# Emission order of attention groups and recurrence steps in an RWKV-7 layer

## The chip, the cores and the metric

One Trainium2 chip; the kernel runs on one of its cores. The metric is the time of one execution on the device, in microseconds (us), as the median of several runs. PE is the matrix engine (its weight loads are listed apart, as PEld), DVE the vector engine, ACT the scalar engine, POOL the general-purpose one, and SP the queue that issues nearly all DMAs here.

## What is computed

The reference runs a first block on a 256 x 1024 input (feed-forward, a mixer of two branches, feed-forward) and then a second block of two layers. The change lies in the mixer of the first block alone:

```python
h = rms_norm(x, mix_norm[l])
p_rwkv, p_q, p_k, p_v, p_gate = _split_last(h @ w_in[l], ...)
y_a = rwkv7_time_mix(p_rwkv, ...)        # a recurrence over 256 steps, 16 heads
y_b = dilated_attention(p_q, p_k, p_v, q_gain, k_gain)   # 3 groups of 4 heads, dilations 1, 4, 16
g_a, g_b = _split_last(jax.nn.sigmoid(p_gate + b_gate[l]), (D_MODEL, D_MODEL))
merged = g_a * (y_a @ w_proj_rwkv[l]) + g_b * (y_b @ w_proj_attn[l])
x = x + merged @ w_out[l]
```

The three attention groups are mixed at the end by a softmax over their log-sum-exp values, so `y_b` is complete only when the third group is. Until both branches are there nothing of them depends on the other.

## The kernel before

All matrices are float32, each split into a high and a low part, so that a product takes three matmuls (`gemm`, L214 to L216, with tokens on the partitions; `gemm_t`, L249 to L251, transposed). `weights` loads a piece, ACT casts its high part (L202) and DVE subtracts for the low one (L203).

The mixer is written as Python generators; each `yield` ends a step, and a string called `PLAN` says whose next step is emitted:

- `0` and `1` are the recurrence of the first and the second half of the heads (`rwkv_half`). Its steps: three of preparation; the Gram products (L689); four that share a chain of 31 pairs of small DVE operations (L718, L720), here s0-4, s5-10, s11-17 and s18-30; the inverse's other blocks (L736, L741); then for each half t of the tokens a step p (L790, L800), a step RG (L815) and two chunk steps ch (L839, L845). ch2 also holds the first normalization. Two more steps, the second normalization with its transposes (L309) and the last transposes, end a half.
- `k` is the second half's keys, `g` the gate chunks (`gate_work`, two of eight chunks a step; its results go to DRAM).
- `a` is `fill`: the attention's values; then for a group g its preparation (a `gemm`, squares, an inverse root by seven to ten tiny DVE operations in a chain, L285 to L290, and transposes, L911) and six steps of a three-stage pipeline over its four heads: `scores` (L923 to L931), `turn` (L937), `values` (L945 to L949). After group 2 come the softmax over groups (L962 to L972) and the transposes of the result (L309); then what is left of `g`, then the attention's projection (`project`, four chunks, L1007).

When the string ends, `for x in "0k1ga"` emits what is left of each, in that order. `last_projection` (the recurrence's projection and `w_out`) follows.

Emission order is a priority, not the order of an engine: the framework under the kernel places the semaphores and fixes each engine's order when the program is built, and lets later work go first where it expects earlier work to wait. The buffers are shared by tag: four PSUM banks `g` for dense products, four `t` for everything else on PE, 21 SBUF slots `q` and 16 slots `h`. Attention scores, masks' sums, gate values and normalization squares are all `h`; scores, transposes, values and every product of the recurrence are `t`. `ada` (L1162) is work for the second block, whose pool takes the memory that the recurrence frees.

Of the kernel before, what the change touches and what calls it, by code (L numbers as in the profile page):

```python
# [18 lines left out]

PLAN = "0000k000aa0000kk0010g010a0111gaa11aaa1aaa111a1aa11aa11a1aa"
P = 128
NQ, NH, NG, NWR, NWS, NS = 21, 16, 4, 4, 3, 2
D = 1024
# [106 lines left out]
class Builder:  # L132
# [890 lines left out]
    def first_block(self, X, nxt):  # L1023
# [29 lines left out]
        with self.inner() as self.ip:  # L1053
# [34 lines left out]
            for hh in range(2):  # L1088
                fills[str(hh)] = self.rwkv_half(hh, S[hh], yT)
            for x in PLAN:  # L1090
                next(fills[x], None)
# [592 lines left out]
```

## Time and profile before

| | us |
|---|---|
| median of 3 runs | 2926.4 (2920.22 to 2927.43) |
| profiled execution, its own time | 2930.7 |
| its span, first to last instruction | 2928.9 |
| PE busy | 2823.6 (96%) |
| DVE busy | 1933.8 (66%) |
| ACT busy | 1176.4 (40%) |
| granted PE clock, mean | 0.978 |

[...] Idle time of an engine counts only where later work waits for it.

### The profile page before, as it was taken

To read this page: it belongs to the slowest core of one execution; us is meant where nothing else is said; L and a number is where in the kernel's file an instruction comes from. 1 tells how busy PE (TensorE), PEld (TensorE's weight loads), DVE (VectorE), ACT (ScalarE), POOL (GpSimd) and SP (SyncE) were. 2 spreads that over 40 slices of the span, in tenths; PEclk is the share of its full clock that TensorE was granted. 3 is DMA by queue.
4 is the path that set the end of the run, shared out by engine and by line. 5 is a ranking of instruction groups with operands and counts; after the bars stand their busy time and mean duration, and the time that the engine had idled before them with its cause. 6 is when DMAs were issued, how large, how long until landed. Compare 5 with 4: busy or idle time off the path is not lost.

```text
span 2928.9 us, 42526 instructions
## 1 busy us (share of the span) xinstructions
PE 2823.6 (96%) x16536; PEld 2407.4 (82%) x16536; DVE 1933.8 (66%) x3478; ACT 1176.4 (40%) x1955; POOL 22.4 (1%) x81
## 2 busy tenths in 40 slices
PE   8999898899999999999999999999999999999998
PEld 7987777688987889877888878787778897799797
DVE  8867887868665544357764597777755456665656
ACT  4445344344444333244523333232334444444443
POOL 0000000000000000000000000000000000000000
PEclk9999897799999999999999999999999999999999
DMA  8756543466651222322152464454432342245564
GB/s 276 232 163 210 174 129 97 138 211 209 194 173 45 70 65 65 103 72 62 46 171 91 157 230 148 157 175 151 156 97 80 101 140 87 87 148 181 165 189 148
DMA packets 298644, 409.59 MB, mean 140 GB/s; under 512 B 31557, under 2 KB 182981, under 8 KB 298442
## 3 DMA queue, kind: packets, MB, share of 16 engines
q1 hardware_dynamic: 298442, 406.87, 43.9%
q8 instruction: 130, 2.13, 0.3%
q14 instruction: 72, 0.59, 0.1%
HBM read 396.98 MB, written 3.24 MB: 137 GB/s over the span
## 4 chain that ended last, share of the span: by engine, by line
PE 80%; DVE 13%; ACT 3%; DMA 2%; issue 2%; SPq 0%; DVEq 0%; ACTq 0%
PE g L215 12%; PE g L216 12%; PE g L214 11%; PE g L249 10%; PE g L251 10%; PE g L250 10%; DVE wl L203 3%; PE dC L1370 2%; PE tr L309 1%; PE I L1346 1%; DVE aa L1162 1%; ACT dae L1467 1%; ACT wh L202 1%; PE ada L1147 1%; PE f L1537 1%
## 5 line engine op out<-in xcount | busy, mean ns | idle before, releaser
L203 DVE TENSOR_TENSOR wl<-wr,wh 128x1024 fp32r<-128x1024 f32 (+1 forms) x606 | 733.1, 1212 | 581.8 <-ACT wh L202 579.6
L202 ACT CAST wh<-wr 128x1024 fp32r<-128x1024 f32 (+1 forms) x606 | 631.3, 1043 | 1056.4 <-PE g L216 490.6
L215 PE MATMUL g<-wl,xh 128*128 128x512 f32 (+2 forms) x1880 | 731.2, 389 | 21.6 <-DVE wl L203 21.0
L214 PE MATMUL g<-wh,xh 128*128 128x512 f32 (+2 forms) x1880 | 729.1, 391 | 5.7 <-ACT wh L202 4.6
L249 PE MATMUL g<-xh,wh 128*128 128x256 f32 (+1 forms) x2352 | 724.9, 308 | 3.2 <-DVE gate L1009 2.5
L216 PE MATMUL g<-wh,xl 128*128 128x512 f32 (+2 forms) x1880 | 726.2, 387 | 0.6 <-DVE xl L297 0.6
L251 PE MATMUL g<-xh,wl 128*128 128x256 f32 (+1 forms) x2352 | 720.7, 307 | 2.6 <-DVE wl L203 2.6
L250 PE MATMUL g<-xl,wh 128*128 128x256 f32 (+1 forms) x2352 | 720.4, 306 | 0.0
L249 PEld LDWEIGHTS g<-xh,wh 128*128 128x128 f32 x2352 | 450.8, 192 | 37.6 <-issue 12.2
L251 PEld LDWEIGHTS g<-xh,wl 128*128 128x128 f32 x2352 | 450.4, 192 | 26.5 <-DVE wl L203 3.4
L250 PEld LDWEIGHTS g<-xl,wh 128*128 128x128 f32 x2352 | 450.8, 192 | 20.9 <-issue 1.3
L215 PEld LDWEIGHTS g<-wl,xh 128*128 128x128 f32 x1880 | 358.7, 191 | 95.2 <-DVE wl L203 28.7
L214 PEld LDWEIGHTS g<-wh,xh 128*128 128x128 f32 x1880 | 355.9, 190 | 86.5 <-issue 9.2
L216 PEld LDWEIGHTS g<-wh,xl 128*128 128x128 f32 x1880 | 358.4, 191 | 72.2 <-DVE xl L297 3.7
L1162 DVE SCALAR_TENSOR_TENSOR aa<-wa,cond,aa 128x512 f32<-128x512 f32 x336 | 232.1, 745 | 6.8 <-DMA wa<-in_w_ada_dram 6.7
L296 ACT CAST xh<-tr 128x256 fp32r<-128x256 f32 (+1 forms) x114 | 50.6, 463 | 132.1 <-PE tr L309 124.0
L1467 ACT ACTIVATE dae<-sc,dast 128x512 f32<-128x512 f32 (+1 forms) x96 | 58.5, 614 | 42.2 <-DVE dast L1465 37.3
L297 DVE TENSOR_TENSOR xl<-tr,xh 128x256 fp32r<-128x256 f32 (+1 forms) x114 | 58.0, 530 | 21.6 <-ACT xh L296 21.3
L1465 DVE TENSOR_REDUCE dast<-sc 128x1 f32<-128x512 f32 (+1 forms) x96 | 53.8, 595 | 24.2 <-PE sc L1464 23.7
L1370 PE MATMUL dC<-vo,kw 128*128 128x257 f32 x192 | 50.3, 394 | 0.0
L309 PE MATMUL tr<-ident,hn 128*128 128x128 f32 x160 | 26.7, 305 | 24.4 <-DVE hn L357 17.5
L1162 DVE SCALAR_TENSOR_TENSOR aa<-wa,cond,ab 128x512 f32<-128x512 f32 x48 | 34.9, 746 | 20.1 <-PE ada L1147 16.7
(387 smaller groups left out, 2537.0 us busy)
## 6 DMA issues: line engine op xcount, KB each, us to landing
wr<-in_w_in_dram SPq DMA_DIRECT2D x156, 512.0 KB
wa<-in_w_ada_dram SPq DMA_DIRECT2D x192, 256.0 KB
wr<-in_ffn_w_in_dram SPq DMA_DIRECT2D x88, 512.0 KB
wr<-in_w_ffn_in_dram SPq DMA_DIRECT2D x84, 512.0 KB
wr<-in_w_in_dram SPq DMA_DIRECT2D x156, 256.0 KB
wr<-in_w_ffn_out_dram SPq DMA_DIRECT2D x50, 512.0 KB
wr<-in_ffn_w_out_dram SPq DMA_DIRECT2D x44, 512.0 KB
wr<-in_w_out_dram SPq DMA_DIRECT2D x32, 512.0 KB
```

Of the source, the lines that this page charges most:

```text
L202: nc.scalar.copy(out=wh[:, :kn, :ntot], in_=src)
L203: nc.vector.tensor_tensor(out=wl[:, :kn, :ntot], in0=src, in1=wh[:, :kn, :ntot].bitcast(F32), op=ALU.subtract)
L214: nc.tensor.matmul(o_, xh, wh[:, n0:n1], start=(kc == 0), stop=False)
L215: nc.tensor.matmul(o_, xh, wl[:, n0:n1], start=False, stop=False)
L216: nc.tensor.matmul(o_, xl, wh[:, n0:n1], start=False, stop=(kc == nk - 1))
L249: nc.tensor.matmul(o_, wh[:, fs], xh, start=(kc == 0), stop=False)
L250: nc.tensor.matmul(o_, wh[:, fs], xl, start=False, stop=False)
L251: nc.tensor.matmul(o_, wl[:, fs], xh, start=False, stop=(kc == nk - 1))
L297: self.nc.vector.tensor_tensor(out=lo, in0=src, in1=hi.bitcast(F32), op=ALU.subtract)
L1162: nc.vector.scalar_tensor_tensor(out=y, in0=raw, scalar=self.cond[:, k, s:s + 1], in1=acc[s], op0=ALU.mult, op1=ALU.add)
L1370: nc.tensor.matmul(pc[:, 0:257], kw[:, kc * P:(kc + 1) * P], V[t][:, 0:257], start=True, stop=True)
L1467: nc.scalar.activation(out=em, in_=ps[:, 0:n], func=AF.Exp, bias=st[:, m:m + 1], scale=1.0, accum_out=st[:, 2 + m:3 + m])
```

## The change

One string is replaced:

```diff
-PLAN = "0000k000aa0000kk0010g010a0111gaa11aaa1aaa111a1aa11aa11a1aa"
+PLAN = "0000k000aa0000kk0010g010a0111gaaaa1aaaa1aaa1aaa1aaa1aaa1aa1a1a11a11"
```

The first 32 letters are the same. Up to there the second recurrence has emitted s0-4 and attention group 1 its preparation. Then, with `1:` for steps of the second recurrence and the rest steps of `a`:

| before | after |
|---|---|
| 1: s5-10, s11-17 | group 0 steps 0, 1 |
| group 0 steps 0 to 2 | 1: s5-10 |
| 1: s18-30 | group 0 steps 2 to 5 |
| group 0 steps 3 to 5 | 1: s11-17 |
| 1: inverse, p (t=0), RG | group 2 preparation, group 1 step 0 |
| group 2 preparation, its products | 1: s18-30 |
| 1: ch0 | group 1 steps 1 to 3 |
| group 2 preparation, its transposes; group 1 step 0 | 1: inverse |
| 1: ch1, p (t=1) | group 1 steps 4, 5; group 2 step 0 |
| group 1 steps 1, 2 | 1: p (t=0) |
| 1: RG, ch2 | group 2 steps 1 to 3 |
| group 1 step 3 | 1: RG |
| 1: ch3 | group 2 steps 4, 5 |
| group 1 steps 4, 5 | 1: ch0; softmax over groups; 1: ch1 |
| (string ends) last steps of 0, then of 1 | transposes of the result, gates 0, 1 |
| gates 0 to 3 | 1: p (t=1), RG; gates 2, 3; 1: ch2, ch3 |
| group 2 steps 0 to 5, softmax over groups | (string ends) last steps of 0, then of 1 |
| transposes of the result, projection | projection |

No instruction is added, removed or changed in shape.

## Rows read from the trace of the kernel before

**Rows 1.** The page: busy time of the engines.
```profile
PE 2823.6 (96%) x16536; PEld 2407.4 (82%) x16536; DVE 1933.8 (66%) x3478; ACT 1176.4 (40%) x1955; POOL 22.4 (1%) x81
```

**Rows 2.** Windows: stretch, length, then busy PE, PEld, DVE, ACT, POOL; clock; DMA.
```profile
428.00:473.50 45.50, 41.71 (x246) 34.33 (x245) 42.31 (x124) 22.04 (x46) 1.04 (x2) 1.00 0.51 150
473.50:482.00 8.50, 7.80 (x150) 7.44 (x152) 6.17 (x7) 1.90 (x5) 0.00 (x0) 0.59 0.57 184
482.00:505.00 23.00, 17.07 (x138) 15.21 (x138) 11.42 (x42) 6.41 (x17) 0.00 (x0) 0.57 0.02 7
505.00:528.00 23.00, 23.00 (x226) 19.09 (x224) 16.67 (x45) 8.87 (x30) 1.00 (x2) 0.91 0.03 8
528.00:552.00 24.00, 18.40 (x108) 13.20 (x107) 23.17 (x55) 10.67 (x23) 0.53 (x1) 0.89 0.62 203
552.00:575.70 23.70, 17.48 (x68) 13.10 (x68) 18.13 (x38) 9.01 (x34) 0.53 (x1) 0.50 0.48 163
575.70:600.20 24.50, 24.47 (x181) 24.01 (x182) 15.22 (x20) 7.25 (x9) 0.00 (x0) 0.89 0.59 181
```

**Rows 3.** Timeline of PE: start, length, line, tiles, count, idle before it and releaser.
```profile
495.99 1.94 PE L911 MATMUL tr<-ident,dsq 128*128 128x128 f32 x8 [5.05 <-DVE drs_y L290]
...
499.44 0.90 PE L839 MATMUL pf<-WV,GB 128*128 128x64 f32 x3
...
551.99 1.12 PE L309 MATMUL tr<-ident,O 128*128 128x128 f32 x4 [0.78 <-DVE O L775]
553.03 0.81 PE L923 MATMUL sc<-qkT 64*128 64x128 f32 x4
...
569.40 0.64 PE L947 MATMUL po<-dv,dpT 128*128 128x64 f32 x2
572.69 2.80 PE L309 MATMUL tr<-ident,dy 128*128 128x128 f32 x12 [2.65 <-DVE dy L972]
575.73 0.79 PE L249 MATMUL g<-xh,wh 128*128 128x256 f32 x2 [0.25 <-ACT xh L296]
```

**Rows 4.** Windows of tile dsc alone: busy PE, PEld, DVE, ACT; clock; DMA.
```profile
428.00:473.50 45.50, 2.84 (x12) 1.52 (x12) 4.97 (x12) 4.30 (x16) 1.00 0.51 150
...
505.00:528.00 23.00, 2.24 (x12) 1.35 (x12) 3.58 (x9) 2.96 (x12) 0.91 0.03 8
...
552.00:575.70 23.70, 4.02 (x12) 2.36 (x12) 4.38 (x12) 3.84 (x16) 0.50 0.48 163
```

**Rows 5.** Windows of tile qkT alone: busy PE, PEld, DVE, ACT; clock; DMA.
```profile
428.00:473.50 45.50, 3.03 (x16) 1.64 (x16) 0.00 (x0) 1.68 (x4) 1.00 0.51 150
...
505.00:528.00 23.00, 2.71 (x12) 1.56 (x12) 0.00 (x0) 0.00 (x0) 0.91 0.03 8
...
552.00:575.70 23.70, 4.96 (x16) 2.79 (x16) 0.00 (x0) 0.00 (x0) 0.50 0.48 163
```

**Rows 6.** Windows of tile po alone: busy PE, PEld, ACT; clock; DMA.
```profile
428.00:473.50 45.50, 3.21 (x24) 3.14 (x24) 1.31 (x8) 1.00 0.51 150
...
552.00:575.70 23.70, 5.86 (x24) 5.63 (x24) 1.31 (x8) 0.50 0.48 163
```

**Rows 7.** Lines on DVE, 485 to 497 us: count, busy us, mean ns, idle before.
```profile
L904 DVE TENSOR_TENSOR dsq<-g,drs_y 128x512 f32<-128x512 f32 x2 | 1.4, 692 | 0.1
L901 DVE TENSOR_REDUCE dms<-dsq 128x8 f32<-128x512 f32 x2 | 1.3, 682 | 0.1
L289 DVE SCALAR_TENSOR_TENSOR drs_w<-drs_w,dms 128x8 f32<-128x8 f32 x6 | 1.0, 162 | 0.0
```

**Rows 8.** Timeline of PE, a gate chunk's first matmul after 458 us.
```profile
460.20 0.28 PE L249 MATMUL g<-xh,wh 128*128 128x256 f32 x1
```

**Rows 9.** Timeline of ACT, the next gate activations after that.
```profile
533.52 2.41 ACT L990 ACTIVATE gate<-g,bg 128x256 f32<-128x256 f32 x6
```

**Rows 10.** Timeline of DVE, the attention's projection: its fourth and last chunk.
```profile
595.82 0.69 DVE L1007 SCALAR_TENSOR_TENSOR merged<-gk,g 128x512 f32<-128x512 f32 x1 [2.08 <-PE g L251]
```

**Rows 11.** Lines on DVE, 552 to 575.7 us: the work for the second block.
```profile
L1162 DVE SCALAR_TENSOR_TENSOR aa<-wa,cond,aa 128x512 f32<-128x512 f32 x13 | 9.4, 740 | 0.0
```

## The prediction

> **What bounds the kernel now.** I read the page first. PE is busy 96% of the span [rows 1], so time can only be won where PE waits or runs slowly, and the change touches only the mixer's second half. I therefore cut the trace into stretches from the second recurrence's chain of DVE pairs to the end of the attention's projection [rows 2]: the DVE chain (428 to 473.5), the inverse (to 482), the first half of the tokens (to 505), the second half (to 528), normalizations and last transposes (to 552), group 2 of the attention (to 575.7), the projection. The reader is to see three things there. In the first stretch DVE is busy 42.31 of 45.5 us: anything added to DVE there lengthens it. From 473.5 on the granted clock falls to about 0.59 and 0.57, comes back, and is 0.50 through all of group 2. And from 482 to 505, and again from 528 to 575.7, PE is not full.
>
> Then I read PE's timeline where it is not full [rows 3]. PE waits 5.05 us for the transposes of group 2's preparation, whose tiny DVE operations come late; behind them the next chunk's products stand (L839, 499.44). At 553.03 group 2's first scores come right behind the last transposes of the second recurrence (551.99), so group 2 begins only when the recurrence is over. Its last product is at 569.40, the softmax over groups and the scaling of the result hold PE 2.65 us, and the projection's first matmul is at 575.73. The fourth chunk of the projection is taken up at 595.82 [rows 10].
>
> So in this part a latency chain (recurrence), a second one (group 2) and dense work (projection) run one after the other. Each leaves PE room that another could use.
>
> **What the change does, and each cost.** Nothing is added or removed, so only places count. Signs are of the total time.
>
> a. Group 2's six steps, the softmax and the transposes leave the end: from 551.99 + 1.12 = 553.11 to 575.73, that is -22.6 us [rows 3]. Nothing dense covers them now, so all of it goes from there. Next late is the last recurrence transposes, after which the recurrence's projection can start.
>
> b. Group 2's preparation leaves the stretch of the first chunks. Its wait of 5.05 us goes, and so do its transposes and first scores, from 495.99 to 499.44: 3.45 us; -8.5 together [rows 3]. Bounds: -8.5, and -5.05 if something else of the attention takes the place of the 3.45.
>
> c. Group 1's later steps leave the second half of the tokens, where PE is busy 23.00 of 23. Their transposes take 2.24 us of PE there and their scores 2.71 [rows 4, 5]: -5. Bounds 0 (a dense chunk fills the room and does not pay for itself) and -5.
>
> d. The projection takes 595.82 - 575.73 = 20.1 us [rows 3, 10]. With `y_b` ready before the second half of the tokens, its matmuls can fill PE in the normalization stretch, where PE is idle 24.0 - 18.4 = 5.6 us [rows 2], and in what c frees. I take -8: that idle time and half of c's. Bounds 0 (it stays behind the recurrence) and -20.1. Its gate values are DMAs back from DRAM on SP; now the gate activations before them come only at 533.52 although a gate chunk's matmuls start at 460.20 [rows 8, 9]: as I read it, the `h` slots are handed out in emission order, and these stand behind the normalizations' squares. In the new order they come ahead of those, so the stores and loads on SP move earlier, past a queue that is nearly empty from 482 to 528 (DMA share 0.02 and 0.03 [rows 2]). No charge.
>
> e. On the other side, the DVE chain gets group 2's preparation (two reductions 1.3, two scalings 1.4, and three lines of six tiny operations of which one line is 1.0 [rows 7]; some 5.7 in all) and the first of group 1's heads: four heads of group 0 took 4.97 on DVE [rows 4], so 1.2. That is 6.9 us into a stretch with 3.2 of slack [rows 2]. Slack in a chain is seldom where one wants it: +7. Bounds +3.7 (all slack used) and +10.7 (all four heads come before the chain ends).
>
> f. The inverse stretch, PE 7.80 of 8.50, gets group 1's PE work. A group at the high clock is 2.84 + 3.03 + 3.21 = 9.1 us of PE [rows 4, 5, 6]. Most of it can lie under the longer DVE chain, where PE needs filling anyway. +4; bounds 0 and +9.1.
>
> g. Group 2's steps now stand between the inverse and the first chunk. At the high clock they cost the same 9.1 us of PE. The recurrence leaves PE and DVE gaps there (5.9 us of PE, of which b has taken 5.05 [rows 2, 3]), so I let nothing of it hide: +9. Bounds 0 (all of it in gaps of the recurrence) and +17.0, the length of the six steps as they stand now, 570.04 - 553.03 [rows 3], if each of their waits is also a wait of the recurrence. At the low clock a group is 4.02 + 4.96 + 5.86 = 14.8 us of PE [rows 4, 5, 6], inside these bounds.
>
> h. The softmax over groups and the transposes go in front of the second half of the tokens. Now that is 575.73 - 570.04 = 5.7 us [rows 3]; PE's part is 2.80, at the low clock. The recurrence's ch1 can run meanwhile. +3; bounds +1.4 (PE's part at the high clock, half of 2.80) and +5.7.
>
> DVE's work for the second block, thirteen operations of 740 ns in group 2's stretch [rows 11], loses a cover. It is wanted only later, and I charge nothing; uncovered it would be at most that 9.4.
>
> Sum: -22.6 - 8.5 - 5 - 8 + 7 + 4 + 9 + 3 = -21.1. Against the profiled execution's own 2930.7 that is 2909.6. The median shown is 2926.4, 4.3 lower, so I forecast 2905 as a median. All good ends together are -22.6 - 8.5 - 5 - 20.1 + 3.7 + 0 + 0 + 1.4 = -51; all bad ones are -22.6 - 5.05 + 0 + 0 + 10.7 + 9.1 + 17.0 + 5.7 = +15.
>
> One row speaks against g above all: L839 at 499.44 needed nothing from the transposes in front of it, and still came after their 5.05 us of waiting [rows 3]. [...] What follows from it for twelve more attention steps ahead of the recurrence is the second rival.
>
> **Rivals.**
>
> 1. The gaps are bought back (no change). Each group 2 step costs its full latency ahead of the recurrence (g = +17.0), and the inverse gets all of group 1's PE work (f = +9.1), while the projection stays behind (d = 0): -22.6 - 8.5 - 5 + 7 + 9.1 + 17.0 + 3 = 0, thus 2926. For it: PE's order is fixed at the build, and a step waits twice for ACT and DVE. Against: group 1's steps stand between recurrence steps now in a stretch where PE is full [rows 2], so interleaving does work at that grain.
>
> 2. Slower. Both groups' twelve steps run ahead of the recurrence at their full latency, because the products of both share PE's order and the four `t` banks, which a step holds while it waits for its exponentials. Price: 17.0 / 6 = 2.8 us a step [rows 3], 34 us for twelve in place of f and g. Sum with d = 0: -22.6 - 8.5 - 5 + 7 + 34 + 3 = +8, thus 2934; with h and e at their ends +14, thus 2941. It decides from 2.8 us a step on; at 2 us a step the sum is -2. For it: the 5.05 us wait shows one case. Against: 2.8 is a step at half the clock with nothing beside it.
>
> 3. Nothing moves. A gate chunk's matmuls run at 460.20, far ahead of their emission place behind the recurrence [rows 8], so the build may order the work by readiness whatever the string says: 2926. Against: group 2's scores come exactly behind the recurrence's last transposes [rows 3], and the gate activations exactly where their `h` slots allow [rows 9], so what uses `t` and `h` does follow the string.
>
> 4. Much faster. The projection lies wholly under the recurrence's end and group 2 mostly in gaps (d = -17, g = +4): 21.1 + 9 + 5 = 35 faster, 2891.
>
> **How the numbers follow.** The forecast's own case (2896 to 2916) has 0.44, rival 4 0.16, rival 1 0.17, rival 2 0.15, rival 3 0.08. The predicted time is the first's, 2905. The range, from the good side of rival 4 to the plain form of rival 2, is 2886 to 2934. A difference of 0.3%, 8.8 us, is about what a measurement can tell from no change: faster than 2917.6 takes the forecast's case, rival 4 and a little of rival 1: 0.62; within the bound most of rival 1, rival 3 and the milder rival 2: 0.22; slower than 2935.2: 0.16.
>
> **What would show it.** Right: group 2's scores (L923) stand before ch0, no PE wait of 5 us for its preparation, the projection's first L1007 comes before or within a few us of the last L309 of the recurrence, and the granted clock is 1.00 in the stretch before the recurrence's projection; the last of the DVE pairs (L720) ends some 7 us later than 473.5, the end of the first stretch, and the recurrence's projection starts about 20 us earlier than now. Step d is wrong if the projection's matmuls all stand behind the last L309; e if the chain of pairs ends more than 11 us later; f and g if the first chunk's state is more than 20 us later than now. The prediction fails on the slow side if PE waits of some 2 us stand before each of group 1's and group 2's transposes (L937) with recurrence products behind them.

## The result, and the profile after

The changed kernel takes 2888.2 us (median of 4 runs, 2884.3 to 2895.6) against 2926.9 for the one before (4 runs, 2920.2 to 2930.1): a ratio of 0.9878, 95% interval 0.9864 to 0.9893; the medians differ by 38.7 us. That lies inside the forecast range, 2 us from its low end of 2886; the forecast was 2905. The profiled execution of the changed kernel, 2895.55 us, is the longest of its four, so the trace shows 35.1 us of the gain (span 2893.8 against 2928.9).

The page's busy line [rows 1 has that of before] and its granted clock, by fortieths of the span:

```profile
PE 2806.5 (97%) x16536; PEld 2393.6 (83%) x16536; DVE 1929.5 (67%) x3478; ACT 1175.6 (41%) x1955; POOL 22.3 (1%) x81
...
PEclk9999899999999999999999999999999999999999
```

The work is the same. PE is busy 17 us less, at a mean granted clock of 0.986 against 0.978. The same stretches as in [rows 2], cut at the same events of the changed trace: DVE's chain of pairs, inverse, first half of the tokens, second half, normalizations, and the start of the recurrence's projection. Group 2 and the attention's projection have no stretch of their own any more.

```profile
428.00:482.40 54.40, 50.70 (x299) 40.90 (x297) 49.80 (x164) 29.32 (x74) 1.04 (x2) 0.97 0.43 129
482.40:494.70 12.30, 12.30 (x196) 10.87 (x195) 6.07 (x9) 5.31 (x14) 0.00 (x0) 0.84 0.47 143
494.70:515.40 20.70, 20.70 (x194) 18.33 (x192) 12.02 (x27) 11.69 (x39) 0.00 (x0) 0.93 0.11 39
515.40:537.00 21.60, 21.12 (x237) 18.49 (x235) 19.14 (x58) 9.22 (x22) 1.00 (x2) 1.00 0.29 93
537.00:560.80 23.80, 23.57 (x169) 20.31 (x168) 22.61 (x47) 9.35 (x13) 0.53 (x1) 1.00 0.80 263
560.80:585.00 24.20, 22.83 (x178) 21.56 (x179) 23.69 (x31) 9.21 (x11) 0.00 (x0) 1.00 0.71 235
```

From the inverse on PE has next to no idle time: 12.30 of 12.30, 20.70 of 20.70, 21.12 of 21.60, 23.57 of 23.80. The normalization stretch is as long as it was (23.8 against 24.0), but now PE is full in it at a clock of 1.00. The timeline of PE says with what (start, length, instruction, idle before it and its releaser):

```profile
468.96 0.66 PE L911 MATMUL tr<-ident,dsq 128*128 128x128 f32 x4 [0.34 <-DVE dsq L904]
...
496.66 2.40 PE L800 MATMUL p<-XA,TT 64*64 64x128 f32 x32
498.99 0.48 PE L923 MATMUL sc<-qkT 64*128 64x128 f32 x2
...
514.32 1.12 PE L845 MATMUL pf<-S,RG 64*128 64x64 f32 x16
519.55 0.71 PE L309 MATMUL tr<-ident,dy 128*128 128x128 f32 x5
...
535.37 1.11 PE L845 MATMUL pf<-S,RG 64*128 64x64 f32 x16
...
560.80 0.66 PE L309 MATMUL tr<-ident,O 128*128 128x128 f32 x4 [0.24 <-DVE O L775]
562.14 0.38 PE L249 MATMUL g<-xh,wh 128*128 128x256 f32 x1 [0.68 <-ACT xh L296]
```

Set beside [rows 3]: group 2's preparation holds PE 0.34 us where it held it 5.05; group 2's scores stand between the recurrence's products (498.99); the attention's result is transposed at 519.55, in front of the second half of the tokens, where that came at 572.69; and behind the recurrence's last transposes (560.80) only the recurrence's projection is left. The gate activations now come at 509 to 528 (ACT's timeline; compare [rows 9]), and the attention's projection is taken up by DVE before those last transposes (DVE's timeline; compare [rows 10]):

```profile
509.33 0.86 ACT L990 ACTIVATE gate<-g,bg 128x256 f32<-128x256 f32 x2
...
527.43 0.47 ACT L990 ACTIVATE gate<-g,bg 128x256 f32<-128x256 f32 x1
```

```profile
548.36 0.68 DVE L1007 SCALAR_TENSOR_TENSOR merged<-gk,g 128x512 f32<-128x512 f32 x1
...
559.48 0.68 DVE L1007 SCALAR_TENSOR_TENSOR merged<-gk,g 128x512 f32<-128x512 f32 x1
```

The common finish line is the first chunk of the recurrence's projection as DVE takes it up (L1009). In the trace of before, then in that of after:

```profile
602.74 0.68 DVE L1009 SCALAR_TENSOR_TENSOR gk<-gk,g 128x512 f32<-128x512 f32 x1
```

```profile
568.96 0.68 DVE L1009 SCALAR_TENSOR_TENSOR gk<-gk,g 128x512 f32<-128x512 f32 x1
```

That is 33.8 us. From there to the end of the span it is 2326.2 us before and 2324.8 after; over all fourteen kernels of this study it is 2322.4 to 2330.1. So nearly all that a kernel wins, it wins in front of this line.

### The profile page after: what moved, and what is told of

It reads as the page before. It is cut to its first block, busy times and chain, and to the rows that moved or that the text cites. A ratio compares the mean times of both kernels' runs of the same rounds, so it can differ in the third digit from the quotient of the medians.

```text
span 2893.8 us, 42534 instructions
## 1 busy us (share of the span) xinstructions
PE 2806.5 (97%) x16536; PEld 2393.6 (83%) x16536; DVE 1929.5 (67%) x3478; ACT 1175.6 (41%) x1955; POOL 22.3 (1%) x81
## 4 chain that ended last, share of the span: by engine, by line
PE 80%; DVE 13%; ACT 3%; issue 2%; DMA 2%; SPq 0%; DVEq 0%; ACTq 0%
PE g L215 12%; PE g L216 12%; PE g L214 11%; PE g L249 10%; PE g L251 10%; PE g L250 10%; DVE wl L203 3%; PE dC L1370 2%; PE tr L309 1%; PE I L1346 1%; ACT dae L1467 1%; PE ada L1147 1%; PE f L1537 1%; DMA mod<-ada 1%; PE f L1528 1%
## 5 line engine op out<-in xcount | busy, mean ns | idle before, releaser
L249 PE MATMUL g<-xh,wh 128*128 128x256 f32 (+1 forms) x2352 | 723.7, 308 | 1.4 <-DVE gate L1009 0.8
L251 PE MATMUL g<-xh,wl 128*128 128x256 f32 (+1 forms) x2352 | 720.1, 307 | 2.4 <-DVE wl L203 2.3
L250 PE MATMUL g<-xl,wh 128*128 128x256 f32 (+1 forms) x2352 | 718.9, 306 | 0.0
L249 PEld LDWEIGHTS g<-xh,wh 128*128 128x128 f32 x2352 | 449.3, 191 | 35.9 <-issue 10.9
L251 PEld LDWEIGHTS g<-xh,wl 128*128 128x128 f32 x2352 | 448.9, 191 | 27.0 <-DVE wl L203 3.9
L250 PEld LDWEIGHTS g<-xl,wh 128*128 128x128 f32 x2352 | 449.1, 191 | 20.8 <-issue 1.6
L309 PE MATMUL tr<-ident,hn 128*128 128x128 f32 x160 | 26.3, 303 | 25.8 <-DVE hn L357 18.8
L1162 DVE SCALAR_TENSOR_TENSOR aa<-wa,cond,ab 128x512 f32<-128x512 f32 x48 | 34.8, 746 | 20.1 <-PE ada L1147 16.7
```

The lines of the kernel that those rows point to most:

```text
L249: nc.tensor.matmul(o_, wh[:, fs], xh, start=(kc == 0), stop=False)
L250: nc.tensor.matmul(o_, wh[:, fs], xl, start=False, stop=False)
L251: nc.tensor.matmul(o_, wl[:, fs], xh, start=False, stop=(kc == nk - 1))
L1162: nc.vector.scalar_tensor_tensor(out=y, in0=raw, scalar=self.cond[:, k, s:s + 1], in1=acc[s], op0=ALU.mult, op1=ALU.add)
```

## The experiments

Times are medians; ratios are to runs of the kernel before on the same chip, with 95% intervals. The columns in the middle are read off each profiled execution, in us from the span's start: the start of the first of DVE's 31 pairs in the second recurrence (its first L720) and the end of the last, the end of ch3 (L845) and of the recurrence's last transposes (L309), and the start of the first L1009.

| kernel | us | ratio | first pair | pairs end | ch3 | transposes | L1009 |
|---|---|---|---|---|---|---|---|
| before | 2926.9 | 1 | 437.1 | 472.4 | 527.3 | 553.1 | 602.7 |
| changed | 2888.2 | 0.9878 (0.9864 to 0.9893) | 437.7 | 480.7 | 536.5 | 561.5 | 569.0 |
| e1 group 2 last | 2921.2 | 0.9988 (0.9979 to 0.9997) | 436.4 | 478.0 | 516.3 | 541.3 | 592.2 |
| e2 gates and transposes last | 2903.5 | 0.9929 (0.9916 to 0.9941) | 437.2 | 478.8 | 526.1 | 548.8 | 576.7 |
| e2b only gates last | 2897.7 | 0.9903 (0.9886 to 0.9921) | 439.9 | 483.1 | 539.6 | 564.0 | 577.4 |
| e3 only the preparation early | 2912.7 | 0.9952 (0.9940 to 0.9964) | 430.2 | 468.6 | 516.1 | 542.5 | 591.8 |
| e5 projection in the string | 2897.0 | 0.9897 (0.9884 to 0.9910) | 434.2 | 477.4 | 530.1 | 560.8 | 569.4 |
| e6 half 0's last steps early | 2899.3 | 0.9903 (0.9890 to 0.9915) | 441.7 | 485.2 | 543.5 | 565.0 | 572.7 |
| e7 group 2 in a lump | 2891.7 | 0.9886 (0.9872 to 0.9900) | 437.3 | 478.9 | 531.7 | 556.8 | 564.3 |
| e8 group 1 later | 2904.1 | 0.9921 (0.9903 to 0.9940) | 437.4 | 474.2 | 536.4 | 562.0 | 569.8 |
| e10 e2b, own gate slots | 2898.1 | 0.9897 (0.9877 to 0.9916) | 447.6 | 487.4 | 542.1 | 561.5 | 575.9 |
| e12 changed, own gate slots | 2895.7 | 0.9897 (0.9879 to 0.9915) | 441.4 | 481.1 | 540.9 | 565.6 | 574.6 |
| e13 before, own gate slots | 2915.7 | 0.9962 (0.9950 to 0.9974) | 434.9 | 466.5 | 521.6 | 539.9 | 589.5 |
| e14 before, PE filled | 2925.9 | 1.0001 (0.9991 to 1.0012) | 436.6 | 471.9 | 526.8 | 553.4 | 602.4 |

Several of the new orders vary more from run to run than the kernel before: e8 from 2894 to 2914, e2b from 2891 to 2909. In both the longest execution is the one with the lowest mean granted clock: e8's shortest has 0.989 and its longest 0.981, e2b's 0.989 and 0.983. The profiled execution of the changed kernel is 7.3 us above its median, that of e2b 11.6 above and that of e8 7.3 below its own, those of e2, e5 and e14 within 1.3 of theirs. So times are compared by the medians, and the middle columns only for where a kernel spends its time. By their intervals e1, e2, e3, e8, e13 and e14 are slower than the changed kernel; those of e2b, e5, e6, e7, e10 and e12 overlap with its own.

The first pairs start up to 10 us away from those of the kernel before and the changed one, and the later columns carry that along. For e3 the cause can be read. Here are the 602 matmuls from the end of the first recurrence's pairs to the end of its last chunk, ahead of everything that e3 moves, first in the trace of before, then in that of e3 (windows as in [rows 2]):

```profile
345.20:404.60 59.40, 58.45 (x602) 49.46 (x600) 40.14 (x78) 24.98 (x46) 0.00 (x0) 0.91 0.47 135
```

```profile
342.60:397.70 55.10, 54.16 (x602) 45.73 (x601) 40.30 (x78) 24.87 (x47) 0.00 (x0) 1.00 0.51 145
```

PE is idle 0.95 us of it in both, and the clock makes 4.3 us. e5 has 55.10 us at 1.00 there, the changed kernel 60.90 at 0.89. e8 makes the same move as e3 at the same place and has 59.60 at 0.91, so nothing ties this to the edit; what sets it is open. Below, where it matters, times are therefore also counted from the first pair on.

All diffs of strings below are against the changed kernel, behind the common first 32 letters, unless it says otherwise.

**What must stand early.** e1, e2 and e2b put parts of the change back, and e3 makes one of its moves alone.

```diff
# e1_group2_last
-aa1aaaa1aaa1aaa1aaa1aaa1aa1a1a11a11
+aa1aaaa1aaa1aaa1aa11111111
# e2_gates_last: the transposes and both gate steps behind the recurrence
-aa1aaaa1aaa1aaa1aaa1aaa1aa1a1a11a11
+aa1aaaa1aaa1aaa1aaa1aaa1aa1a11111
# e2b_only_gates_last: one string, and one line at the end of dilated()
-aa1aaaa1aaa1aaa1aaa1aaa1aa1a1a11a11
+aa1aaaa1aaa1aaa1aaa1aaa1aa1a1a1111
         self.yB = yT
+        yield
# e3_prep_early: against the kernel before
-11aaa1aaa111a1aa11aa11a1aa
+11aaa1aaaaa1111a11aa11a1aa
```

> Group 2's six steps, the softmax over groups, the result's transposes and the gates 0 to 3 are emitted behind the recurrence, as before; group 2's preparation and all of group 1 stand early, as in the changed kernel. Theory (the gain is group 2 leaving the end and the projection then filling the recurrence's end): 2918 to 2928, for the chain of DVE pairs ends some 8 us later, the wait of 5 us goes, and group 2 and the projection stand in series at the end again. Rival (the gain is the recurrence's own stretch: the preparation's wait gone, higher clock): 2895 to 2908.

> As the changed kernel, but the transposes of the attention's result and the gates 0 to 3 are emitted behind the recurrence. Theory: group 2's 22.6 us mostly stay won, but the projection waits for those transposes and stands in series again, so some 20 us of the gain go: 2903 to 2914, first projection matmul behind the last transposes of the recurrence. Rival (the projection is hidden by something else, or hardly counts): 2886 to 2893.

> As the changed kernel, but only the gates 0 to 3 are emitted behind the recurrence; the transposes of the attention's result keep their place. Theory that the gates' place among the h slots matters: their activations come behind the normalizations' squares again, they hold all four dense PSUM banks until then, and the projection starts some 10 us later: 2892 to 2902. Rival (the early transposes alone do it): 2885 to 2891.

> The kernel before with one move: group 2's preparation (two steps) is emitted right behind group 0's last step, ahead of the inverse; all else as before. Theory: PE's wait of 5 us goes and DVE's chain is hardly touched: 4 to 9 us faster, 2918 to 2923. Rival (the recurrence's stretch is where the gain was): 2900 to 2910. A third reading, that the wait was hidden by others: 2926.

e1 came out as the theory said (2921.2 in 2918 to 2928), and e2 at the fast edge of its theory (2903.5 in 2903 to 2914). In e1 the recurrence is over 12 us sooner than in the kernel before, and then group 2's scores start; from the last transposes to the first L1009 it is 50.9 us, where it was 49.6. In e2 the same gap is 27.9, and in the changed kernel 7.5. The timelines of PE around the end of the recurrence, first e1, then e2:

```profile
540.16 1.11 PE L309 MATMUL tr<-ident,O 128*128 128x128 f32 x4 [3.56 <-DVE O L775]
541.20 0.81 PE L923 MATMUL sc<-qkT 64*128 64x128 f32 x4
```

```profile
547.66 1.12 PE L309 MATMUL tr<-ident,O 128*128 128x128 f32 x4 [2.88 <-DVE O L775]
548.57 2.53 PE L309 MATMUL tr<-ident,dy 128*128 128x128 f32 x12
551.56 0.51 PE L249 MATMUL g<-xh,wh 128*128 128x256 f32 x2 [0.46 <-ACT xh L296]
```

So 12 transposes of 2.53 us, left behind the recurrence, keep the whole projection behind it. It is also to be seen that the recurrence itself ends at 548.8 in e2 and at 561.5 in the changed kernel, so what is taken out of series is paid back in part. Most of these 12.7 us, 10.4, are there at the end of ch3 (526.1 against 536.5), when the projection has hardly begun: they come with the transposes and gates that the changed kernel puts between the chunks. The normalizations, which lie over the projection, take 2.3 us longer (25.0 against 22.7).

e2b costs 9.5 us of the gain by the medians, inside what I expected if the gates' place mattered, but its interval overlaps with that of the changed kernel; more of it below. e3 missed its theory (4 to 9 us) on the fast side and its rival on the slow one: by the medians, moving two steps alone is worth 13 us. The preparation's transposes stand at 461.84 and 463.73, PE's wait of 5.05 us is gone (the longest left between p and ch1 is 0.42), and the state's products of ch1 start at 489.12 where they did at 503.04:

```profile
461.84 0.38 PE L911 MATMUL tr<-ident,dsq 128*128 128x128 f32 x2
463.73 0.60 PE L911 MATMUL tr<-ident,dsq 128*128 128x128 f32 x4
```

```profile
482.24 1.11 PE L815 MATMUL p<-GB,Ta 64*64 64x128 f32 x22 [0.42 <-ACT Ta L803]
...
489.12 1.11 PE L845 MATMUL pf<-S,RG 64*128 64x64 f32 x16
```

That is 13.9 us at ch1, but 7.0 of them were there at the first pair, so 7.0 are e3's own, against the 8.5 of term b. At the first L1009 3.9 us are left, counted in the same way (161.7 against 165.6). So of the 13 us this trace puts some 4 in the stretch that the edit touches; where the rest comes from is not shown. In e1, where group 1's steps stand ahead of ch1 as well, 3 us of the 7.0 are left there.

The wait is not all that went. From p (L800) to the end of ch1, before and in e3:

```profile
483.65:505.01 21.36, 16.31 (x126) 14.61 (x128) 10.73 (x41) 5.87 (x16) 0.00 (x0) 0.58 0.00 1
```

```profile
479.43:490.23 10.80, 10.38 (x128) 9.37 (x129) 7.01 (x16) 3.26 (x7) 0.00 (x0) 1.00 0.01 2
```

About as many matmuls keep PE busy 10.4 us at a clock of 1.00, where they took 16.3 at 0.58. So the wait of 5.05 us and the clock each make about half of the 10.6 us. Whether the move kept the clock up, or this execution had it so, one trace can't tell.

**Where attention steps are cheapest.** Four other orders of the full interleaving:

```diff
# e5_projection_in_plan
-aa1aaaa1aaa1aaa1aaa1aaa1aa1a1a11a11
+aa1aaaa1aaa1aaa1aaa1aaa1aa1a1a11a11aa
# e6_half0_early
-aa1aaaa1aaa1aaa1aaa1aaa1aa1a1a11a11
+aa1aaaa1aaa1aaa100aaa1aaa1aa1a1a11a11
# e7_group2_lump
-aa1aaaa1aaa1aaa1aaa1aaa1aa1a1a11a11
+aa1aaaa1aaa1aaa1aaaaaaaa111a1a11a11
# e8_group1_later
-aa1aaaa1aaa1aaa1aaa1aaa1aa1a1a11a11
+11aaa1aaaaa1aaa1aaa1aaa1aaa1aa11a11
```

> The changed kernel with the projection's two steps emitted ahead of the recurrences' last normalizations instead of behind them. Theory (the build already pulls the projection's matmuls in front, since only h slots and PSUM banks hold it back): within 6 us of the changed kernel, 2882 to 2894. Rival (emission place decides, dense work ahead of the normalizations' transposes delays the end): 2895 to 2905.

> The changed kernel with the last two steps of half 0 emitted right behind the second recurrence's inverse, not at the end. Theory (the end of the recurrence, 25 us with DVE full, is now the chain in front of the recurrence's projection, and half of its DVE work is half 0's): 5 to 12 us faster than the changed kernel, 2876 to 2883. Rival (that end is set by PE's dense work, which stays): 2886 to 2890.

> The changed kernel with group 2's six steps emitted in one lump ahead of p for the first tokens, not spread over p, RG and ch0. This measures the price of a step that nothing of the recurrence covers. Theory (spread steps lie in the recurrence's gaps): the lump exposes some 1 to 1.5 us a step, 5 to 9 us slower than the changed kernel, 2893 to 2897. Rival (a step costs its PE work wherever it stands): 2886 to 2890.

> Group 2's preparation right behind group 0 as in the run that moved it alone; then groups 1 and 2 spread three steps at a time over inverse, p, RG, ch0 and ch1; softmax, transposes and gates 0, 1 behind ch1, gates 2, 3 behind RG of the second tokens. So the chain of DVE pairs is spared group 1. Theory (e was a true cost of 7 us, and moving the preparation alone gave 13): 4 to 10 us faster than the changed kernel, 2878 to 2884. Rival (DVE's work is only moved behind the chain, where it costs the same): 2886 to 2892.

None beats the changed kernel. e7 falls between its two readings: 3.5 us by the medians, with overlapping intervals. So a lump of six steps costs at most little more than six spread ones. In its windows PE is full both over the inverse and the lump and over the chunks behind, at a clock of 1.00; a step's waits are filled with dense matmuls. (Its trace is even 4.7 us ahead of that of the changed kernel at the first L1009; the changed one ran at 0.84 from 482.4 to 494.7.)

```profile
478.90:503.40 24.50, 24.10 (x304) 21.78 (x302) 15.45 (x28) 14.02 (x42) 0.00 (x0) 1.00 0.31 101
503.40:518.00 14.60, 14.05 (x183) 13.20 (x183) 10.85 (x24) 6.67 (x17) 0.00 (x0) 1.00 0.21 73
```

e6 and e8 came out slower than both of their readings. e8 does spare the DVE chain (474.2 against 480.7), but ch3 ends at 536.4 against 536.5: group 1 has given it all back. e6 shortens the normalizations to 21.5 us and pays for it ahead: ch3 is 7.0 us later, 3.1 of them behind the first pair, and from the first pair to the first L1009 it takes 131.0 us, the changed kernel 131.2. In its windows, from the inverse up to p, and over the normalizations, PE is full in both:

```profile
485.20:509.00 23.80, 23.26 (x288) 20.35 (x287) 16.55 (x31) 10.36 (x21) 0.00 (x0) 1.00 0.41 124
543.50:565.00 21.50, 21.30 (x159) 18.99 (x157) 20.62 (x41) 8.75 (x12) 0.63 (x2) 1.00 0.88 279
```

That much is what a bound by work and not by waits looks like: what leaves one stretch turns up in the next. By the medians e8 is 16 us slower than the changed kernel; the two profiled executions are about equal (span 2895.0 against 2893.8), so the traces don't show where these 16 us go.

e5 was expected within 6 us and took 8.7 more, by the medians, inside its rival's range (2895 to 2905). Where it pays is to be seen: ch3 comes 6.4 us sooner than in the changed kernel, 3.6 of them from ahead of the first pair, and then the normalization stretch takes 30.7 us, not 25.0, with DVE busy in 29.64 of them:

```profile
530.10:560.80 30.70, 27.50 (x188) 23.21 (x186) 29.64 (x60) 9.92 (x14) 0.65 (x2) 0.94 0.73 233
```

**Gates and their slots.** Two slots of their own, in memory that this stage has spare, for the mixer's gate values:

```diff
# e12_changed_own_slots; e10 is the same on e2b, e13 on the kernel before
-            th = self.h([P, 512], F32, "gate")
+            th = self.h([P, 512], F32, "gate") if bias is None else self.ip.tile([P, 512], F32, tag="gs", bufs=2, name="gate")
```

> As the run with only the gates 0 to 3 emitted last, but the mixer's gate values have two slots of their own instead of h slots. Theory (behind the recurrence they waited for h slots, and so held the dense PSUM banks): their activations come some 20 us earlier than in that run, the projection starts earlier, 2884 to 2892. Rival (the emission place itself, as priority, made that run slower): as that run, 2894 to 2901.

> The changed kernel with the same two slots of their own for the mixer's gate values. Theory (in the changed kernel the gates already get h slots before anything waits for their banks): no change beyond 4 us, 2884 to 2892. Rival (h slots still hold it back): 2878 to 2883.

> The kernel before with the same two slots of their own for the mixer's gate values. Theory (early gates only make room on PE, and with group 2 behind the recurrence there is nothing to fill it): 2918 to 2928, the recurrence perhaps some us earlier. Rival (the early gates alone bring much of the gain): 2898 to 2912.

e13 shows that the late activations of [rows 9] were due to the `h` slots: with slots of their own the first two come at 467.26, and the recurrence ends 13.2 us sooner, 11.0 counted from the first pair. Both readings were off: 10.8 us, more than the theory allowed and less than the rival. Group 2 still starts when the recurrence is over, and from there to the first L1009 it is the same 49.6 us as before.

```profile
467.26 0.83 ACT L990 ACTIVATE gate<-g,bg 128x256 f32<-128x256 f32 x2
...
528.94 0.83 ACT L990 ACTIVATE gate<-g,bg 128x256 f32<-128x256 f32 x2
```

```profile
539.24 0.66 PE L309 MATMUL tr<-ident,O 128*128 128x128 f32 x4 [0.78 <-DVE O L775]
539.83 0.50 PE L923 MATMUL sc<-qkT 64*128 64x128 f32 x4
```

In the new order slots bring nothing by the medians: e10 is no faster than e2b (2898.1 against 2897.7), inside its rival's range. The first activations come 64 us sooner, but the last chunk's are still at 549.58, as I read it because its matmuls keep the priority of their late place, and the projection's first product is taken up at 556.5, in e2b at 556.9. ACT's timeline in e10, whose lines behind the added `yield` are numbered one higher; in e2b there was one group of eight at 545.69:

```profile
481.24 0.83 ACT L991 ACTIVATE gate<-g,bg 128x256 f32<-128x256 f32 x2
...
529.41 0.83 ACT L991 ACTIVATE gate<-g,bg 128x256 f32<-128x256 f32 x2
549.58 0.83 ACT L991 ACTIVATE gate<-g,bg 128x256 f32<-128x256 f32 x2
```

But that does not settle what the slots do. e10's first pair comes 7.7 us behind that of e2b (granted clock from 400 to 430 us 0.78 against 0.94), and from there to the first L1009 it takes 128.3 us against 137.5. So in these traces the slots would bring some 9 us where they were meant to, and the time is lost ahead; whether by the slots of gates 4 to 7, which stand there, or by the clock alone, was not tested.

e12 is 7.4 us slower than the changed kernel by the medians, above both of its readings, their intervals overlapping. It is no gain in any case: from the first pair to the first L1009 it takes 133.2 us against 131.2.

**Is there room on PE, and what does the clock cost?** The kernel before, with extra matmuls; nobody reads their results:

```diff
# e14_before_filled_pe
+    def warm(self, n):
+        p = self.g()
+        for _ in range(n):
+            self.nc.tensor.matmul(p[:, 0:256], self.mixT.toks(0, 0, P)[0], self.mixT.toks(1, 0, 256)[0], start=True, stop=True)
...
+            if hh and t:
+                self.warm(10)
             pg = self.t("pg")
...
+            if it["at"][0] == 2:
+                self.warm(10)
             p = self.t("tr")
...
+            if g == 2:
+                self.warm(10)
             ps = self.t("sc")
...
-        xT = keep.pop()
+        xT = self.mixT = keep.pop()
```

> The kernel before with extra matmuls whose results nobody reads, ten in front of each of group 2's score and turn products and of each last normalization's product: only PE's load is changed. Theory (group 2's stretch is a chain through PE, ACT and DVE, and the clock is a smaller part of its 22.6 us): granted clock near 1.00 there, group 2's own PE work near 9.1 us in place of 14.8, the stretch within 4 us of what it was, 2922 to 2931. Rival (the low clock makes most of the stretch): the stretch 5 us shorter or more, 2915 to 2921.

The time is the same, but the test turned into another one: the build pulled the extra matmuls ahead of group 2, 74 of the 90 in the trace into the normalization stretch. Windows of the normalizations and of group 2, to be held against [rows 2]:

```profile
528.00:552.00 24.00, 24.00 (x177) 20.96 (x177) 23.29 (x55) 10.18 (x22) 0.53 (x1) 1.00 0.64 199
552.00:575.70 23.70, 17.08 (x78) 13.27 (x77) 19.34 (x41) 9.28 (x34) 0.53 (x1) 0.61 0.56 179
```

So what it settles is term d: in the kernel before, the normalization stretch takes 69 more matmuls (177 against 108) on PE, which is then full at a clock of 1.00, and the last transposes end 0.3 us later than without them. DVE is busy 23.29 of the 24.00 us (23.17 in the kernel before): the recurrence's end runs through it, and PE's room under it is free. (These matmuls load and split no weights, so they say nothing of the DVE work that comes with the projection's.) What group 2's stretch would have lasted at a clock of 1.00 was not tested.

## Why the prediction held, and where it was small

The direction and the mechanism were the ones forecast, the size was not: the forecast's own case, 2896 to 2916, did not happen, and 2888.2 lies in the range because its good end was taken from the fourth rival, which had 0.16. That the range held is partly luck. What was right: group 2 leaves the end, and the projection, which waited for it, goes under the recurrence. By the events of the two profiled executions:

| step | forecast | measured | how |
|---|---|---|---|
| e, DVE's pairs end later | +7 | +8.3 | 480.7 - 472.4 |
| f, from there to p (L800) | +4 | +4.7 | 15.97 - 11.26 |
| b and g, from p to the end of ch1 | +0.5 | -2.6 | 18.78 - 21.36 |
| c and h, to the end of ch3 | -2 | -1.2 | 21.04 - 22.25 |
| normalizations | 0 | -0.9 | 24.98 - 25.85 |
| a and d, from the last transposes to the first L1009 | -30.6 | -42.1 | 7.5 - 49.6 |
| sum | -21.1 | -33.8 | |

Another 1.3 us of the span lie behind that line, and 3.6 more between the profiled executions and the medians.

**Step d is the term that was mis-sized.** With a at -22.6, d is -42.1 + 22.6 = -19.5, where I took -8 of at most 20.1. I had counted PE's idle 5.6 us in the normalization stretch and half of what c frees. Two things were wrong in that. Of the 108 matmuls that kept PE busy 18.4 us there, 75 (25 each at L249, L250 and L251) belonged to gates, and the gates go to earlier gaps when they are emitted ahead of the normalizations. And part of PE's busy time there goes with the clock, which is 1.00 from 528 to 546, 0.70 from 546 to 548 and 0.50 from 548 to 552 in the trace of before: the same four products (L773, L774) take 1.85 us longer in its second part than in its first.

```profile
529.90 1.02 PE L773 MATMUL pg<-g,lg 128*128 128x512 f32 x2
530.85 1.12 PE L774 MATMUL pg<-g2b,lg 32*128 32x512 f32 x2
...
547.29 1.92 PE L773 MATMUL pg<-g,lg 128*128 128x512 f32 x2
549.13 2.07 PE L774 MATMUL pg<-g2b,lg 32*128 32x512 f32 x2
```

e14 filled the stretch with 69 more matmuls at no cost, at 1.00. Shown by e2: with only transposes and gates put back, 15.3 of 38.7 us are lost by the medians, and the projection stands in series (551.56). e2b puts 9.5 of it on the gates alone, by medians whose intervals overlap; whether through the `h` slots is open. The split of -42.1 takes a at its forecast size; only their sum is measured.

**Steps e and f were right in size**, e in part by luck. I had one of group 1's four heads under the DVE chain, and all four came there, the case of my bound +10.7: the scores' tile takes twice what it took for group 0 alone [rows 4].

```profile
428.00:480.69 52.69, 4.94 (x21) 2.67 (x21) 9.42 (x24) 8.12 (x32) 0.97 0.41 125
```

Yet DVE's busy time up to the chain's end rose by 7.2 only (48.42 from 41.23), so other work left it. And e8 shows that e is not a loss one can save: the DVE chain ends 6.5 us sooner, and ch3 no sooner. They are places at which work is paid that has to be paid somewhere.

**Steps b and g** came out better together by 3.1 us: PE is full from 494.7 to 515.4, with no wait for an attention step, so the steps lie in the recurrence's gaps or under dense matmuls. A second cause has no term in the sum: the clock, which was 0.58 from p to the end of ch1 and is now

```profile
496.66:515.44 18.78, 18.78 (x185) 16.64 (x184) 11.37 (x26) 11.57 (x37) 0.00 (x0) 0.98 0.12 43
```

so that 59 more matmuls cost PE 2.5 us more busy time (18.78 from 16.31). e3 alone, with 128 matmuls at 1.00, won 10.6 there, 5.05 of it the wait. How much of -2.6 is gaps and how much clock was not separated.

**Step h's good bound** took PE's part, 2.80 us in a stretch at 0.50, to halve at the high clock, an estimate. Measured, the twelve transposes of `dy` keep PE busy 1.63 us in the changed kernel, at 1.00 (515.4 to 537).

**The rivals.** The first and second needed attention steps that hold up the recurrence; the windows show PE busy 33.00 of 33.00 us from 482.4 to 515.4, and e7's lump of six costs 3.5 us by the medians, not 17. In the kernel before, what stood behind matmuls with late operands did come late: L839 at 499.44, behind the 5.05 us of [rows 3]. In the new order group 2's preparation holds PE 0.34 us, and from 482.4 to 515.4, where dense matmuls stand between the attention steps, PE waits for nothing. The third is out: L923 went ahead of the first chunk (498.99; the first L839 comes at 509.82). The fourth, 2891, is what happened, nearly by its own numbers (d = -17, measured -19.5; b and g together -4.5, measured -2.6).

What stays open: in which stretch e8 loses its 16 us; what makes the granted clock, and with it the time of the new orders, differ from run to run; whether the late gates of e2b cost their 9.5 us by their slots; and what group 2's stretch would have taken at a clock of 1.00.

## What to carry to other kernels

Read the end of a branch for what it holds back. Group 2's stretch was worth its own 22.6 us, but it also kept 20 us of dense work in series that could have run under a latency chain; count both. When you estimate how much fits under a chain, don't take an engine's busy time in that stretch as its load: part of it may move out with the same edit (here 75 of 108 matmuls), and part of it may be a low clock (here 0.50 from 548 to 552). And once PE was busy over nine tenths of every stretch of the region, moving steps inside it won nothing: four further orders were no better. When you compare traces, look first at a stretch that the edit cannot have touched: in e3 it differed by 7 us.

## What the chip showed that I had not expected

The granted clock fell with PE busy all the time. In the changed kernel PE is busy 12.30 of 12.30 us from 482.4 to 494.7 and the clock is 0.84 there on average; behind the inverse's 32x32 matmuls (L736, L741, up to 490.1) it is 0.58, where it was 1.00 from 482.4 to 490.0:

```profile
490.00:495.00 5.00, 5.00 (x49) 4.07 (x47) 1.40 (x4) 1.89 (x7) 0.00 (x0) 0.58 0.64 184
```

In the kernel before it was 0.59 from 473.5 to 482 with PE busy 7.80 of 8.50 [rows 2]. So the busy time in the trace does not tell when the clock falls. What a higher clock gives depends on what bounds the stretch: in e14 it rose from 0.89 to 1.00 in the normalization stretch, where DVE is full (23.17 and 23.29 of 24.00 us), and the last transposes came no sooner (553.4 against 553.1); in the first recurrence, where PE is full (58.45 of 59.40 us in the kernel before), 602 matmuls took 55.1 us at 1.00 and 59.4 at 0.91.
